# A hybrid decoder step on one core: when v is requested and used in the recurrence, and where small tiles and first triangles travel

## The chip, the core and the metric

The kernel runs on one core of a Trainium2 chip. The metric is device time in microseconds of one execution. A profiled execution leaves a trace with every instruction of the five engines: TensorE (PE, with its weight loads as PEld), VectorE (DVE), ScalarE (ACT), GpSimd (POOL), and SyncE (SP), which here only issues transfers (DMAs). ScalarE issues transfers too, in its own instruction order.

## The reference, cut to what matters

Two layers are computed, for a prompt of 2048 tokens with 16 learned meta tokens ahead, and for 8 short samples of 4 tokens. Layer 0 is sliding-window attention. Layer 1 is RWKV-7 time mixing with 16 heads of 64 channels, whose recurrence is, per token:

```
S = S * w_t + (S a_t) b_t^T + v_t k_t^T          # state, 64 x 64 per head
y_t = S r_t
...
y = (y - mean) * rsqrt(var + GN_EPS) * ln_g + ln_b      # per head
bonus = sum(r * k * r_k) * v
out = ((y + bonus) * silu(g)) @ w_out
```

The bonus is one number per token and head times v; it is added after the group norm.

## The kernel before, in words

The work is written in three phases: attention, the projections of the RWKV layer (their results go to DRAM), and the recurrence. The changes lie in the recurrence, which starts at some 1600 us.

**Units and chunks.** The recurrence runs over 17 units in order: unit 0 holds the meta tokens (one chunk of 32 tokens), units 1 to 16 hold 128 prompt tokens each, in four chunks of 32. Per chunk, `chain` (L1422) does on TensorE the products of the state Z with L (C<-Z,L), ScalarE copies them (R0s), the `solve` (L1394) multiplies by the inverted triangles TT (C<-R0s,TT), ScalarE writes the result into Z, TensorE multiplies by the keys LS (C<-Z,LS), and VectorE multiplies by the decay products `pe` and so writes the state of the next chunk (Z<-C,pe, L1464). These steps depend on each other in a ring. Half of each Z tile holds v of the chunk, loaded by SP two chunks ahead (`load_v`, L1367).

**What is made ahead.** For a unit two places later, `scores` (L948) multiplies BK with L into triangles LAs, `inverse` (L976) sends LAs to DRAM (la_d), loads it rearranged (LA) and inverts it in 31 small steps on GpSimd (X and XT), sends the result to DRAM (tt_d), and `load_TT` (L1334) brings it back as TT. `keys` (L1374) transposes BK on TensorE and ScalarE copies the result into LS. `load_BK` (L894) loads two tiles of 512 KB, `load_L` (L901) two halves of 256 KB for two chunks. The pool of L has six places, that of BK four.

**What follows behind.** `outputs` (L1465) forms y of two chunks (Y). `group_norm` (L1583) is a generator that does the group norm and the bonus of the previous unit in pieces, each ended by a mark. Its first piece requests v (vt<-v, two transfers on SP). Its second takes the mean of the first half and multiplies both vt tiles by the bonus (L1602, vt<-vt,bont). Further pieces subtract the mean, form the variance (VectorE sums, GpSimd's power of -1/2), and scale. `gate` (L1641) and `project_out` (L1684) are dense products that fill TensorE.

**The order of the work.** For units 2 to 14 the function `steady` (L1765) writes out for each of the four chunks which pieces are emitted in which order. At its end `in_order` (L1752) ties VectorE's, ScalarE's and GpSimd's instructions to the order in which they were written. The order of TensorE and SP is chosen by the framework's planner at build time, from simulated times; at run time every engine and queue goes strictly in order.

In chunk 3, `steady` creates the group norm of the unit and runs two pieces of it:

```
                else:
                    norms_[u.idx] = group_norm(u)
                    run(norms_[u.idx], to=MARK)
                    run(norms_[u.idx], to=MARK)
                run(pe[ch], 1.9)
                next(rec, None)
```

The last line emits C<-Z,LS and Z<-C,pe of the chunk. In chunks 0 to 2 the group norm of the previous unit advances by two marks each. BK and L are loaded through ScalarE's queue (`s_`): L of the first two chunks at the end of chunk 3 of the unit before (L1841, kept in `L0s`), BK and the other L at the end of chunk 0 (L1834).

The first three units (`PRE` = 3) are prepared by `elementwise` (L1340) and, for units 1 and 0, inside the projection phase. The small tiles `pe` and `bont` are loaded by `small_loads` (L1319) and lie in the pool `wk`, which belongs to the recurrence phase and takes room that the phase before has used; the pool `wp` (L660) is opened earlier and lives longer.

Of the kernel before, what the change touches and what calls it, by code (L numbers as in the profile page):

```python
# [10 lines left out]
F32 = mybir.dt.float32  # L11
# [3 lines left out]
ALU = mybir.AluOpType  # L15
# [4 lines left out]
P = 128  # L20
D = 1024
KC = 8
# [8 lines left out]
def tile_hybrid_step(ctx: ExitStack, tc: tile.TileContext, a, o, c):  # L31
    nc = tc.nc
    v_, s_, g_, t_ = nc.vector, nc.scalar, nc.gpsimd, nc.tensor
# [9 lines left out]
    def tt(e, out, in0, in1, op):  # L43
        return e.tensor_tensor(out=out, in0=in0, in1=in1, op=op).ins  # L44
# [4 lines left out]
    def dma(out, in_, eng=None):  # L49
        return (eng or nc.sync).dma_start(out=out, in_=in_).ins  # L50
# [192 lines left out]
    with ExitStack() as ph:  # L243
# [403 lines left out]
        n, off = ntok(NT), place[NT][1]  # L647
# [226 lines left out]
    def all_of(gen):  # L874
        for _ in gen:
            pass
# [17 lines left out]
    def load_BK(u, eng=None):  # L894
        u.BK, u.L = [], []
        for half in range(2):
            BK = es.tile([P, 4, 4, 64], F32, name="BK", tag="BK", bufs=nbuf["BK"])
            dma(BK, bk_d[u.blk][:, half * 4:half * 4 + 4, u.c0:u.c0 + u.nch, :], eng)
            u.BK.append(BK)
# [76 lines left out]
    def inverse(u, room=None, ln=None):  # L976

        nch = u.nch
        nl = nch * 16
        la_d = dramr.tile([2, nl // 2, 32, 32], F32, name="la_d", tag=f"la_d{nch}")  # L980
        u.tt_d = tt_d = dramr.tile([32, 4, 4 * nch * 32], F32, name="tt_d", tag=f"tt_d{nch}")
        for e in range(2):
            dma(la_d[e].rearrange("l j i -> j l i"),
                u.LAs[32 * e:32 * e + 32].rearrange("p h c g i -> p (h c g) i"))
        eng = v_ if u.idx == 1 else g_
        if u.kind == "m":
            room = wl.tile([P, 2, 32 * 32], F32, name="roomm", tag="L", bufs=nbuf["L"])
        if room is not None:
            LA = room[:, 0].rearrange("p (j i) -> p j i", i=32)
            XX = room[:, 1].rearrange("p (a k i) -> p a k i", a=2, i=32)  # L990
        else:

            LA = wk.tile([P, 32, 32], F32, name="LA", tag="LA", bufs=2)
            XX = None
        if XX is None:
            X = wk.tile([P, 16, 32], F32, name="X", tag="X", bufs=2)
            XT = wk.tile([P, 16, 32], F32, name="XT", tag="XT")
        else:
            X, XT = XX[:, 0], XX[:, 1]
        if ln is None:  # L1000
            ln = wp.tile([P, 32], F32, name="ln", tag=("mu", "rst0")[u.idx % 2])
        if nch < 4:
            g_.memset(LA, 0.0)
            g_.memset(ln, 1.0)
        for hh in range(2):
            dma(LA[hh * 64:hh * 64 + nl], la_d.rearrange("e l j i -> (e l) j i"))
            dma(ln[hh * 64:hh * 64 + nl], ln_d[u.idx].rearrange("q c g i -> (q c g) i"))
        tt(eng, LA, LA, ln.unsqueeze(2).broadcast_to([P, 32, 32]), ALU.mult)
        dma(X, c["laneid"])

        low = 16 if u.kind == "m" else 0

        part = {2: 16}.get(u.idx, 0)
        cut = [(v_, 0, part), (g_, part, 16)] if 0 < part < 16 else [(v_, 0, 16)] if part else [(eng, 0, 16)]
        for j in range(low, 31):
            if j in (8, 16, 22, 26):
                yield
            w = 3 - j % 4 if u.kind == "s" else 31 - j
            for eng, k0, k1 in cut if w else ():
                ks = slice(max(low // 2, k0), min(j // 2 + 1, k1))  # L1020
                shape = [P, ks.stop - ks.start, w]
                if shape[1] <= 0:
                    continue
                tt(eng, XT[:, ks, :w], LA[:, j:j + 1, j + 1:j + 1 + w].broadcast_to(shape), X[:, ks, j:j + 1].broadcast_to(shape), ALU.mult)
                tt(eng, X[:, ks, j + 1:j + 1 + w], X[:, ks, j + 1:j + 1 + w], XT[:, ks, :w], ALU.add)
        for eng, k0, k1 in reversed(cut):
            u.inverted = tt(eng, X[:, k0:k1], X[:, k0:k1], ln[:, None, :].broadcast_to([P, k1 - k0, 32]), ALU.mult)
        for hh in range(2):
            dma(tt_d[hh:32:2].rearrange("k q (l i) -> (q l) k i", i=32), X[hh * 64:hh * 64 + nl])
# [238 lines left out]
    with ExitStack() as ph:  # L1268
# [50 lines left out]
        def small_loads(u):  # L1319
            if u.kind == "s":  # L1320
                room = wp.tile([P, 192], F32, name="TTs", tag="l1_0")
                u.TT = room[:, 0:128].rearrange("p (c g i) -> p c g i", c=1, i=32)
                u.pe = room[:, 128:192].rearrange("p (g c) -> p g c", c=8)
            else:
                u.pe = wk.tile([P, KC, u.nch], F32, name="pe", tag="pe", bufs=4)
            dma(u.pe, pe_d[u.idx])
            if u.kind != "m":
                u.bont = wk.tile([P, 16], F32, name="bont", tag="bont", bufs=4)
                dma(u.bont[:u.n], bo_d[u.idx])

        def new_LAs(u):
# [80 lines left out]
        def run(gen, budget=None, to=None):  # L1412

            with released():
                while budget is None or budget > 0:
                    x = next(gen, None)
                    if x is None or (x == MARK and to == MARK):
                        return
                    if budget is not None and x != MARK:
                        budget -= x  # L1420
# [162 lines left out]
        def group_norm(u):  # L1583
# [12 lines left out]
            for x in range(2):  # L1596
                ms_ = mean[:n, x * 8:x * 8 + 8]
                v_.tensor_reduce(out=ms_, in_=u.Y[x][:n], axis=AX.X, op=ALU.add)
                v_.tensor_scalar(out=ms_, in0=ms_, scalar1=1.0 / 64, scalar2=None, op0=ALU.mult)
                if vts and x == 0:  # L1600
                    for e in range(2):
                        tt(v_, vts[e], vts[e], u.bont[:n, 8 - e * 8:16 - e * 8].unsqueeze(2).broadcast_to([n, 8, 64]), ALU.mult)  # L1602
                    yield MARK
                if x == 0:
                    u.ytm = u.Ys if u.kind == "s" else lt.tile([P, 2, 8, 64], F32, name="ytm", tag="ytm", bufs=1)
                    y = u.ytm[:n].rearrange("p e g d -> p (e g) d")
                for e, ps_ in HS:
                    if u.kind == "s" and e == 0:
                        tt(v_, u.ytm[:n, x], u.Y[x][:n], ms_.unsqueeze(2).broadcast_to([n, 8, 64]), ALU.subtract)
                    elif u.kind != "s":  # L1610
                        tt(v_, u.ytm[64 * x:64 * x + 64, e], u.Y[x][ps_],
                           mean[ps_, x * 8:x * 8 + 8].unsqueeze(2).broadcast_to([64, 8, 64]), ALU.subtract)
                yield MARK if vts and x == 0 else 2.3
# [6 lines left out]
            with tc.high_priority(offset=5000):  # L1620
                g_.tensor_scalar(out=var[:n], in0=var[:n], scalar1=1.0 / 64, scalar2=64e-5, op0=ALU.mult, op1=ALU.add)
                tt(g_, var[:n], var[:n], mhalf[:n], ALU.pow)
            yield MARK
            tt(v_, y, y, bc(var), ALU.mult)
            yield MARK
# [139 lines left out]
        def steady(i, u, pe):  # L1765
# [9 lines left out]
            for ch in range(4):  # L1775
# [36 lines left out]
                run(pe[ch], 1.2)  # L1812
                next(rec)
                with released():
                    if ch == 0 and i > 2:
                        all_of(keys(u, 1))
                    if ch == 3:
                        all_of(kt)
                        inv[s.idx] = inverse(s)
                        next(inv[s.idx])  # L1820
                    else:
                        next(inv.get(i + 1, idle()), None)
                if ch < 3:
                    run(norm, to=MARK)
                else:
                    norms_[u.idx] = group_norm(u)
                    run(norms_[u.idx], to=MARK)
                    run(norms_[u.idx], to=MARK)
                run(pe[ch], 1.9)
                next(rec, None)  # L1830
                with released():
                    if ch == 0:
                        first = L0s.pop(s.idx, None)
                        load_BK(s, s_)  # L1834
                        s.L.append(first or load_L(s, 0, s_))
                        s.L.append(load_L(s, 1, s_))
                        small_loads(s)
                    if ch == 2 and i + 1 in inv:
                        load_TT(us[i + 1])
                    if ch == 3 and i + 3 < len(us):  # L1840
                        L0s[i + 3] = load_L(us[i + 3], 0, s_)  # L1841
                run(pe[ch], to=MARK)
                rests.append(pe[ch])
                for part in PLAN.get((i, ch), ()):
                    with released():
# [214 lines left out]
```

## Time and profile before

| what | us |
|---|---|
| median of 3 runs | 2597.73 (2594.54 to 2601.28) |
| the profiled execution, its own time | 2601.98 |
| its span in the trace | 2600.2 |
| TensorE busy | 2238.5 (86%) |
| VectorE busy | 1687.0 (65%) |
| ScalarE busy | 1169.5 (45%) |
| GpSimd busy | 1044.8 (40%) |

The shares are means over phases with different limits. The page's slices show it: in the first 60% of the span TensorE stands at 9 tenths or more in most slices, and in the recurrence, from slice 25 on, at 5 to 8 tenths:

```
span 2600.2 us, 60852 instructions
PE   6999999899999898999999997567777777777897
POOL 4242123222112335433333333147566666656613
PEclk9999999999999998999999998778898988889999
```

In the rows below, "idle before <-X" in brackets is the time in which an engine had nothing to do just before the instruction, and what ended it. "issue" means that the profile shows nothing that the engine waited for. SPq and ACTq are transfers being issued by SP and ScalarE; the time is that of the issue, not of the transfer. Neighbouring instructions of one kind are merged into a row with their count.

### The profile page before, as it was taken

How to read it: one execution, taken by the hardware profiler on the slowest of the kernel's cores; microseconds unless marked ns; L12 is line 12 of the kernel's file. 1: busy time of each engine (PE TensorE's matmuls, PEld its weight loads, DVE VectorE, ACT ScalarE, POOL GpSimd, SP SyncE). 2: the span in 40 equal slices, each digit the busy share in tenths (PEclk: the TensorE clock that was granted, in tenths of full speed). 3: DMA queues.
4: the chain of work that ended last, by engine and by line, in shares of the span. 5: the costliest groups of instructions: out<-in, count | busy, mean ns of one | idle time of the engine just before them, and what ended most of it. 6: DMA issues, size and time to landing. Idle time of an engine off the chain costs nothing.

```text
span 2600.2 us, 60852 instructions
## 1 busy us (share of the span) xinstructions
PE 2238.5 (86%) x24932; PEld 1547.7 (60%) x24932; DVE 1687.0 (65%) x3181; ACT 1169.5 (45%) x2799; POOL 1044.8 (40%) x1572
## 2 busy tenths in 40 slices
PE   6999999899999898999999997567777777777897
PEld 5877777767845446676666785354444444444553
DVE  7586675567749887665656665645666566666684
ACT  6676455555523335454434444233443434434432
POOL 4242123222112335433333333147566666656613
PEclk9999999999999998999999998778898988889999
DMA  8433122331447664322222216564544545454423
GB/s 202 122 106 117 63 69 94 107 115 62 150 138 226 210 205 153 98 81 96 86 102 85 93 67 192 140 182 118 132 105 114 135 115 131 103 126 124 106 67 76
DMA packets 346235, 312.99 MB, mean 120 GB/s; under 512 B 205546, under 2 KB 282218, under 8 KB 344131
## 3 DMA queue, kind: packets, MB, share of 16 engines
q1 hardware_dynamic: 327219, 278.03, 36.4%
q10 hardware_dynamic: 17120, 27.27, 4.0%
q0 software_dynamic: 1616, 3.79, 0.7%
q8 instruction: 196, 3.21, 0.5%
q14 instruction: 84, 0.69, 0.1%
HBM read 191.15 MB, written 119.84 MB: 120 GB/s over the span
## 4 chain that ended last, share of the span: by engine, by line
PE 50%; DVE 18%; issue 10%; ACT 9%; DMA 8%; POOL 4%; SPq 2%; POOLq 0%; ACTq 0%; DVEq 0%
PE pd L38 29%; PE po L38 5%; PE C L38 5%; DVE xm L47 4%; DMA BK<-bk 2%; DVE xpr L44 2%; ACT ssb L41 2%; PE pz L38 2%; SPq L50 2%; PE Y L38 2%; PE sc L38 1%; PE oT L38 1%; DMA wst<-in_rwkv_w_in 1%; DMA L<-ar 1%; PE kt L1385 1%
## 5 line engine op out<-in xcount | busy, mean ns | idle before, releaser
L38 PEld LDWEIGHTS <-yp 128*128 128x128 f16 x1488 | 141.1, 99 | 165.2 <-issue 12.8
L47 DVE SCALAR_TENSOR_TENSOR xm<-dx,mu,xn 128x256 f32<-128x256 f32 (+2 forms) x432 | 199.8, 523 | 48.9 <-POOL dx L44 47.6
L44 POOL TENSOR_TENSOR X<-X,XT 128x126 f32<-128x126 f32 (+24 forms) x458 | 202.4, 442 | 35.5
L44 POOL TENSOR_TENSOR XT<-LA,X 128x126 f32<-128x126 f32 (+24 forms) x458 | 180.4, 394 | 39.7 <-DVE X L44 6.0
L38 PE MATMUL C<-Z,L 128*32 128x64 f32 x2048 | 49.5, 247 | 170.4 <-issue 159.9
L38 PE MATMUL pd<-xp,wq 128*128 128x256 f16 (+2 forms) x1728 | 186.0, 266 | 11.4 <-DVE qp L47 8.0
L38 PE MATMUL pd<-wg,xg 128*128 128x512 f16 (+1 forms) x816 | 193.1, 384 | 0.7 <-issue 0.7
L38 PE MATMUL po<-wo,yp 128*128 128x512 f16 x768 | 188.9, 389 | 0.0
L38 PE MATMUL pd<-wvv,xpr 128*128 128x512 f16 (+1 forms) x816 | 187.4, 387 | 0.0
L38 PE MATMUL pd<-xpr,w 128*128 128x256 f16 (+2 forms) x1728 | 186.0, 267 | 0.0
L38 PE MATMUL pd<-xp,wg 128*128 128x256 f16 (+2 forms) x1728 | 182.6, 266 | 0.9 <-DVE xp L44 0.5
L38 PE MATMUL pd<-xpr,wkk 128*128 128x256 f16 (+2 forms) x1728 | 179.5, 264 | 0.0
L38 PEld LDWEIGHTS <-wq 128*128 128x128 f16 x1728 | 159.3, 99 | 32.7 <-DVE qp L47 9.2
L44 POOL TENSOR_TENSOR ssb<-ssb,bias 128x512 f32<-128x512 f32 x64 | 86.4, 1355 | 223.9 <-DVE ssb L462 185.5
L38 PEld LDWEIGHTS <-w 128*128 128x128 f16 x1728 | 157.5, 99 | 27.0 <-issue 9.7
L38 PEld LDWEIGHTS <-wg 128*128 128x128 f16 x1728 | 159.2, 99 | 21.5 <-issue 4.0
L38 PEld LDWEIGHTS <-wkk 128*128 128x128 f16 x1728 | 158.2, 98 | 15.6 <-issue 0.4
L38 PE MATMUL pd<-w,yp 128*128 128x512 f16 x720 | 162.9, 384 | 3.3 <-DMA yp<-y 3.3
L44 POOL TENSOR_TENSOR ps<-wst,ps 128x1024 f16<-128x1024 f32 x32 | 69.5, 2171 | 220.0 <-ACT wst L41 201.7
L38 PEld LDWEIGHTS C<-Z,L 128*32 128x32 f32 x2048 | 38.9, 126 | 195.8 <-issue 192.3
L41 ACT ACTIVATE R0s<-C 128x256 f32<-128x256 f32 x65 | 25.0, 385 | 274.9 <-PE C L38 269.9
L38 PEld LDWEIGHTS <-xpr 128*128 128x128 f16 (+1 forms) x816 | 79.1, 100 | 102.6 <-issue 17.5
(357 smaller groups left out, 4913.2 us busy)
## 6 DMA issues: line engine op xcount, KB each, us to landing
wst<-in_rwkv_w_in SPq DMA_DIRECT2D x32, 512.0 KB
wsp<-ps SPq DMA_DIRECT2D x32, 512.0 KB
x<-in_x_prompt SPq DMA_DIRECT2D x29, 512.0 KB
xn<-xn SPq DMA_DIRECT2D x14, 1028.0 KB
ar<-aro SPq DMA_DIRECT2D x28, 512.0 KB
bk<-bko SPq DMA_DIRECT2D x28, 512.0 KB
BK<-bk ACTq DMA_DIRECT2D x26, 512.0 KB
L<-ar ACTq DMA_DIRECT2D x52, 256.0 KB
```

The source lines that it names most:

```text
L38: return t_.matmul(out=out, lhsT=lhsT, rhs=rhs, start=start, stop=stop, **kw).ins
L41: return s_.activation(out=out, in_=in_, func=func, **kw).ins
L44: return e.tensor_tensor(out=out, in0=in0, in1=in1, op=op).ins
L47: v_.scalar_tensor_tensor(out=out, in0=in0, scalar=scalar, in1=in1, op0=op0, op1=op1)
L50: return (eng or nc.sync).dma_start(out=out, in_=in_).ins
L1385: t_.transpose(out=ps[:w * 64, j].rearrange("p e d -> p (e d)"), in_=u.BK[half][:, j, 2 * c2:2 * c2 + w, :].rearrange("p c x -> p (c x)"), ...
```

## The change

Six things are edited.

1. The two multiplications of vt by the bonus leave the second piece of `group_norm` and form a piece of their own behind the variance's power and ahead of the scaling.
2. `steady` creates the group norm of a unit and runs its first piece (the request for v) at the end of chunk 2 instead of in chunk 3; chunk 3 runs one piece, and at the end of chunk 0 one more piece of the previous unit's norm is run, which is the new one.
3. BK and the first L of the unit two places later are loaded in chunk 0 through SP, between the transposes of the keys and their copies, instead of through ScalarE at the end of chunk 0. The second L stays with ScalarE.
4. The lines that load the first L of a later unit (`if ch == 3 and i + 3 < len(us)`) keep their indentation and so come to lie inside `if ch == 2`.
5. `pe` and `bont` get places in the pool `wp` instead of `wk`.
6. For units 0 to 2 the transfers la_d<-LAs and LA<-la_d are issued by ScalarE instead of SP.

```diff
@@ inverse
         for e in range(2):
             dma(la_d[e].rearrange("l j i -> j l i"),
-                u.LAs[32 * e:32 * e + 32].rearrange("p h c g i -> p (h c g) i"))
+                u.LAs[32 * e:32 * e + 32].rearrange("p h c g i -> p (h c g) i"), s_ if u.idx < PRE else None)
...
         for hh in range(2):
-            dma(LA[hh * 64:hh * 64 + nl], la_d.rearrange("e l j i -> (e l) j i"))
+            dma(LA[hh * 64:hh * 64 + nl], la_d.rearrange("e l j i -> (e l) j i"), s_ if u.idx < PRE else None)
@@ small_loads
-                u.pe = wk.tile([P, KC, u.nch], F32, name="pe", tag="pe", bufs=4)
+                u.pe = wp.tile([P, KC, u.nch], F32, name="pe", tag="pe", bufs=4)
...
-                u.bont = wk.tile([P, 16], F32, name="bont", tag="bont", bufs=4)
+                u.bont = wp.tile([P, 16], F32, name="bont", tag="bont", bufs=4)
@@ group_norm
                 if vts and x == 0:
-                    for e in range(2):
-                        tt(v_, vts[e], vts[e], u.bont[:n, 8 - e * 8:16 - e * 8].unsqueeze(2).broadcast_to([n, 8, 64]), ALU.mult)
                     yield MARK
...
                 tt(g_, var[:n], var[:n], mhalf[:n], ALU.pow)
+            yield MARK
+            for e, vt in enumerate(vts):
+                tt(v_, vt, vt, u.bont[:n, 8 - e * 8:16 - e * 8].unsqueeze(2).broadcast_to([n, 8, 64]), ALU.mult)
             yield MARK
             tt(v_, y, y, bc(var), ALU.mult)
@@ steady
                 with released():
-                    if ch == 0 and i > 2:
-                        all_of(keys(u, 1))
+                    if ch == 0:
+                        kt = keys(u, 1) if i > 2 else idle()
+                        next(kt, None)
+                        first = L0s.pop(s.idx, None)
+                        load_BK(s)
+                        s.L.append(first or load_L(s, 0))
+                        all_of(kt)
...
                 else:
-                    norms_[u.idx] = group_norm(u)
-                    run(norms_[u.idx], to=MARK)
                     run(norms_[u.idx], to=MARK)
                 run(pe[ch], 1.9)
                 next(rec, None)
                 with released():
                     if ch == 0:
-                        first = L0s.pop(s.idx, None)
-                        load_BK(s, s_)
-                        s.L.append(first or load_L(s, 0, s_))
                         s.L.append(load_L(s, 1, s_))
                         small_loads(s)
                     if ch == 2 and i + 1 in inv:
                         load_TT(us[i + 1])
+                if ch == 2:
+                    norms_[u.idx] = group_norm(u)
+                    run(norms_[u.idx], to=MARK)
                     if ch == 3 and i + 3 < len(us):
                         L0s[i + 3] = load_L(us[i + 3], 0, s_)
                 run(pe[ch], to=MARK)
+                if ch == 0:
+                    run(norm, to=MARK)
```

## Rows read from the trace of the kernel before

**Rows 1.** Waits from 1700 to 2400 us: engine, line, releaser, total us, times, longest.

```profile
POOL LA L44 <- DMA LA<-la_d: 120.2, 13, 33.6
DVE vt L44 <- DMA vt<-v: 116.1, 26, 7.7
POOL var L1621 <- DVE var L1618: 76.2, 11, 7.7
```

**Rows 2.** Windows, one unit: length, busy PE, PEld, DVE, ACT, POOL; PEclk, DMA, GB/s.

```profile
2019.80:2072.60 52.80, 39.60 (x762) 24.53 (x760) 32.94 (x50) 21.20 (x54) 33.75 (x69) 0.90 0.48 122
```

**Rows 3.** Chain of waits in order of time, 1560 to 2560: start, us, what.

```profile
1716.65 12.21 DMA L<-ar
...
1808.64 9.06 issue
...
2344.12 8.02 issue
```

**Rows 4.** Timeline of all engines around one unit's end: start, us, engine, instruction.

```profile
2013.02 1.35 SPq L50 DMA_DIRECT2D tt_d<-X  x2
...
2014.48 1.91 SPq L50 DMA_DIRECT2D LA<-la_d  x2
...
2017.67 1.09 SPq L50 DMA_DIRECT2D TT<-tt_d  x2
...
2018.39 1.15 PE L38 MATMUL C<-Z,LS 128*64 128x64 f32 x32
...
2019.27 0.66 SPq L50 DMA_DIRECT2D out_y_prompt<-h  x1
...
2020.31 2.01 DVE L44 TENSOR_TENSOR vt<-vt,bont 128x512 f32<-128x512 f32 x1 [2.93 <-DMA vt<-v]
...
2029.45 0.79 DVE L44 TENSOR_TENSOR vt<-vt,bont 128x512 f32<-128x512 f32 x1 [7.13 <-DMA vt<-v]
...
2030.17 1.72 DVE L44 TENSOR_TENSOR Z<-C,pe 64x256 f32<-64x256 f32 x4
...
2030.69 0.32 SPq L50 DMA_DIRECT2D h<-h  x1
...
2031.99 1.08 PE L38 MATMUL C<-Z,L 128*32 128x64 f32 x32 [10.40 <-issue]
...
2034.70 0.82 PE L38 MATMUL C<-R0s,TT 32*32 32x64 f32 x32
```

**Rows 5.** Timeline of TensorE, matmuls: the first product of successive chunks.

```profile
1749.20 0.65 PE L38 MATMUL C<-Z,L 128*32 128x64 f32 x32
...
1759.01 0.65 PE L38 MATMUL C<-Z,L 128*32 128x64 f32 x32 [0.58 <-PE pd L38]
...
1770.77 0.65 PE L38 MATMUL C<-Z,L 128*32 128x64 f32 x32 [1.55 <-issue]
...
2205.25 0.65 PE L38 MATMUL C<-Z,L 128*32 128x64 f32 x32 [1.55 <-issue]
...
2215.32 0.65 PE L38 MATMUL C<-Z,L 128*32 128x64 f32 x32
...
2225.10 0.65 PE L38 MATMUL C<-Z,L 128*32 128x64 f32 x32
```

**Rows 6.** Timeline of GpSimd: starts of the inverse's first step.

```profile
1760.00 2.28 POOL L44 TENSOR_TENSOR LA<-LA,ln 128x1024 f32<-128x1024 f32 x1 [33.61 <-DMA LA<-la_d]
...
1805.37 1.91 POOL L44 TENSOR_TENSOR LA<-LA,ln 128x1024 f32<-128x1024 f32 x1 [6.76 <-DMA LA<-la_d]
...
2394.75 1.91 POOL L44 TENSOR_TENSOR LA<-LA,ln 128x1024 f32<-128x1024 f32 x1 [6.98 <-DMA LA<-la_d]
```

**Rows 7.** Timeline in chunk 0 and 1 of a steady unit: BK's issue and use.

```profile
2040.34 0.37 ACTq L50 DMA_DIRECT2D BK<-bk  x1
...
2047.69 0.69 PE L38 MATMUL pz<-L,BK 64*64 64x64 f32 x32 [1.26 <-DMA BK<-bk]
```

**Rows 8.** Timeline of VectorE at the recurrence's start.

```profile
1653.74 1.73 DVE L44 TENSOR_TENSOR Z<-C,pe 64x256 f32<-64x256 f32 x4 [7.97 <-DMA pe<-pe]
```

## The prediction

> **What bounds the kernel now.** I read the waits first, summed over the stretch in which most of the recurrence's steady units run [rows 1]. VectorE's multiplication of v by the bonus (vt<-vt,bont) waits 116.1 us for its transfer, 26 times, and GpSimd stands 120.2 us for LA and 76.2 us for VectorE's variance. One unit by the windows [rows 2]: in 52.8 us TensorE is busy 39.60, VectorE 32.94, GpSimd 33.75. No engine is full; what ends a unit is an order.
>
> The chain of waits in order of time shows the place [rows 3]: once a unit TensorE stands in "issue", from 9.06 us at 1808.64 to 8.02 us at 2344.12, 11 such pieces, 8 to 12 us each. The timeline of one such end of a unit explains it [rows 4]. The last LS products of chunk 3 end at 2019.54 (2018.39 + 1.15). VectorE could then make the next Z, but it works in written order, and ahead of Z<-C,pe stand the two bonus multiplications: the first waits 2.93 us and starts at 2020.31, the second waits 7.13 us and starts at 2029.45. Only then comes Z (2030.17, first piece), and with it the next unit's first chunk (C<-Z,L at 2031.99).
>
> Where vt happened to be in time, the same boundary is short [rows 5]: chunk 3 starts at 1749.20 and the next unit at 1759.01, 9.81 us. Chunk 0 then takes 11.76 (to 1770.77), chunk 1 10.07 and chunk 2 9.78 (2205.25, 2215.32, 2225.10). A unit of TensorE without the stand is 9.81 + 11.76 + 10.07 + 9.78 = 41.4 us, waits for BK included.
>
> GpSimd has a loop of its own, one triangle inverse a unit [rows 6]. LA starts at 1760.00 and 1805.37: 45.4 us, a loop in which the variance was not waited for. From 1805.37 to 2394.75 eleven loops take 589.4, 53.58 each; they hold the variance wait, 76.2 / 11 = 6.9 us [rows 1]. Without it they are 46.7. So GpSimd cannot do a unit in less than 45.4 to 46.7 us as long as LA's load stands on SP behind tt_d<-X, the end of the previous inverse (2013.02, then 2014.48) [rows 4]; the wait for that load was 6.76 us in the short loop too.
>
> **The change, part by part.**
>
> *v later and requested sooner.* The bonus multiplications leave the end of chunk 3 for the end of the next unit's chunk 0, behind Z; the request for v goes from the end of chunk 3 to the end of chunk 2. Of the old place only the mean remains ahead of Z. So 11 stands of about 10 us go: Z can start at about 2019.6 and take 1.7 us, the next unit starts near 2021.6 instead of 2031.99, 10.4 us sooner. At the new place v has had a whole chunk 3 and chunk 0, over 20 us, against the 10 us and a little that its second half now takes (requested just ahead of the output row's issue at 2019.27, used at 2029.45) [rows 4]. The two instructions cost VectorE 0.79 us each when alone and 2.01 beside GpSimd's LA product; their cover is VectorE's idle 19.9 us of 52.8, some 13 of 46 afterwards [rows 2, 4].
>
> *What is late next.* TensorE's loop falls to 41.4, GpSimd's to 46 (the middle of 45.4 and 46.7: the variance comes 10 us sooner and is no longer waited for). GpSimd is slower, and its result reaches TensorE: X's end lets tt_d go (2013.02), TT is loaded at 2017.67, and the solve of the next unit's chunk 0 reads it, now at 2034.70. With the next unit at 2021.6 that solve comes by 2024.3: still after TT in the first such unit, but GpSimd loses 46.0 - 41.4 = 4.6 us a unit, so from the second on TensorE waits there for TT. I take 46.0 a unit: 11 x (53.58 - 46.0) = 83 us.
>
> *The page "SBUF — State Buffer" of the Trainium skill, section "Who interferes with whom", speaks against this part:* a VectorE instruction with two inputs in SBUF and a GpSimd instruction that reads SBUF block each other, the later one for the whole of the earlier. The 2.01 us beside the LA product agrees. By that rule the moved pair falls among GpSimd's steps; what this would give is priced as a rival from rows.
>
> *BK and the first L.* They go from ScalarE's queue to SP's, ahead of the copies of the keys instead of behind. The prefetch of the first L at the end of the previous unit is moved under a condition that cannot hold (chunk 3 inside chunk 2), so it is gone: L's 0.5 MB is now loaded in chunk 0 beside BK's 1 MB and the second L's 0.5 MB. Now BK is issued 8.35 us after the unit's start (2040.34 against 2031.99) and the scores wait 1.26 us for it at 2047.69 [rows 4, 7]. Lower bound of the change: -1.3 us a unit (no wait left). Upper: unit 2 loads both L and BK in chunk 0 today, and L lands 12.21 us after its issue [rows 3]; issued 8.35 us after the start at the latest, that is 20.6 against a need at 11.8, an 8.8 us wait a unit. I take 2 us, near the row of the ordinary unit since SP issues about 1 us sooner; TensorE's loop becomes 43.4, still under 46, so nothing is added. The cover is the wait for TT; gone that, it costs those 2 us. ScalarE sheds four issues a unit, worth nothing (it is not the bound).
>
> *Places of their own, first triangles on ScalarE's queue.* The first decay products arrive 7.97 us late at VectorE (1653.74) [rows 8]. A place that shares no earlier tile lets them be fetched long before; behind that wait stand the transfer of Z's v half and TT, so 0 to 8 us, I take 4. The triangles of units 0 to 2 leave SP's queue; between nothing and some of the same 8 us, taken as inside it. From the third unit on both edits are at nothing.
>
> Sum: 83 + 4 = 87 us from the profiled execution's 2601.98 (span 2600.2): 2515. The median of the runs, 2597.73, is 0.16% below that execution; on its scale 2510.
>
> **Rivals.**
>
> 1. *TensorE bounds, LA gets ahead of tt_d.* The order on SP is planned anew. With the scores 10 us sooner, LA's triangle is in DRAM well before X ends, and if LA's load is put first, the 7 us wait goes and GpSimd's loop is about 39. Then TensorE's 41.4 to 43.4 counts, say 42: 11 x 11.6 + 4 = 131 us, 2467. Against it: in the short loop the triangle was early too, and LA still waited 6.76 us [rows 6].
>
> 2. *GpSimd's steps stand behind the moved pair.* Two multiplications of 0.79 us held against its chain make its loop 46.0 + 1.6 = 47.6: 11 x 6.0 + 4 = 70 us, 2528. For it: the 2.01 us in rows 4 show the two engines holding each other. Against: the 45.4 and 46.7 already hold such meetings.
>
> 3. *The transfers of chunk 0 bound.* L as in unit 2, an 8.8 us wait in place of 1: 41.4 - 1.0 + 8.8 = 49.2: 11 x 4.4 + 4 = 52 us, 2542. Without the 4 and at a still later L it ends near 2597, no change.
>
> 4. *Slower: BK and L stand behind h on SP.* The load of h waits until the previous output row is out: issued 2019.27, h at 2030.69 [rows 4]. With the next unit at 2021.6 that is 9.1 us into it, and BK and L now queue behind it. By their tile shapes h, xg, Z's v, BK and both L are 3.25 MB; at unit 2's pace (2 MB in 12.2 us) 19.8 us, so landing 28.9 us into the unit against a need at 11.8: a 17.1 us wait, loop 57.5, 11 x 3.9 = 43 us slower, 2641. It decides from a wait of 13.2 us (53.58 - 40.4). Against it: v's 0.5 MB and L's 0.5 MB leave the very stretch in which that output row is slow, and TensorE's wait for TT gives time back.
>
> **How the numbers follow.** Forecast 0.49 (its own range 2498 to 2524, from loops of 45.4 to 46.7 and 0 to 8 us at the start), rival 1 0.20, rival 2 0.10, rival 3 0.12, rival 4 0.06, no change in effect 0.03. About 0.3% (8 us) is what runs of this kernel can tell from no change. Faster by more: 0.49 + 0.20 + 0.10 + 0.12 = 0.91; within 0.03; slower 0.06. The range takes in the forecast, rivals 1 and 2 and most of 3: 2455 to 2560.
>
> **What would show it.** Right: the wait of vt for v gone from VectorE; the 11 long "issue" pieces gone; LA starts on GpSimd 45 to 47 us apart with the variance not waited for; a new wait of the chunk-0 solve for TT of some 3 us. Rival 1: LA issued ahead of tt_d and a loop near 42. Rival 2: a 46 us chain stretched by steps of over 1 us beside vt. Rivals 3 and 4: long waits of the scores for BK or L. The prediction is wrong if units stay above 49 us or fall under 43.

## The result and the profile after

The changed kernel takes 2566.14 us (median of 4 runs, 2564.59 to 2570.74), the kernel before, on the same chip, 2596.14 (2592.95 to 2601.28): ratio 0.9886, 95% interval 0.9864 to 0.9907. It is 30 us faster; 87 were forecast, and the time lies 6 us above the range. The profiled executions have spans of 2562.7 us and 2600.2.

The waits from 1700 to 2400 us, columns as in [rows 1]:

```profile
POOL LA L44 <- DMA LA<-la_d: 73.2, 7, 11.8
...
PEld pz L38 <- issue: 55.4, 18, 5.9
PE pz L38 <- DMA BK<-bk: 49.7, 17, 5.5
...
PE C L38 <- DMA TT<-tt_d: 26.7, 17, 2.7
...
POOL ms L1704 <- ACT po L41: 13.1, 6, 3.2
```

VectorE's wait of vt is gone, and so is GpSimd's for the variance. What is new stands on TensorE: the scores wait for BK (the weight loads beside them show the same time as "issue"), and the solve waits for TT. GpSimd's wait for LA is larger than this row says: six more of its starts are put down to other transfers that landed last, or to "issue". For the scores' wait for BK the same view of the kernel before has this:

```profile
PE pz L38 <- DMA BK<-bk: 9.1, 8, 2.3
```

The starts of the inverse on GpSimd, first and last of twelve on the changed kernel's timeline, answer to [rows 6]:

```profile
1811.64 1.91 POOL L44 TENSOR_TENSOR LA<-LA,ln 128x1024 f32<-128x1024 f32 x1 [9.24 <-DMA LA<-la_d]
...
2359.18 1.92 POOL L44 TENSOR_TENSOR LA<-LA,ln 128x1024 f32<-128x1024 f32 x1 [8.18 <-issue]
```

Eleven loops take 547.5 us, 49.8 each, where 53.6 were and 46.0 forecast; the wait ahead of them is 10.3 us on average (7.3 before). 11 x 3.8 = 42 us came from the loops; the first of these starts is 6.3 us later than in [rows 6], and the stretch behind the last takes some 2 us less: 37.5 in the spans.

One unit's end by the timeline of all engines of the changed kernel answers to [rows 4] (the last row is the scores of the next unit's chunk 1):

```profile
2142.79 1.55 ACT L41 ACTIVATE LAs<-pz 32x256 f32<-32x256 f32 x4 [0.91 <-PE pz L38]
...
2144.88 1.46 SPq L50 DMA_DIRECT2D Z<-v  x1
2146.44 0.97 SPq L50 DMA_DIRECT2D la_d<-LAs  x2
2146.59 1.64 POOL L44 TENSOR_TENSOR X<-X,ln 128x512 f32<-128x512 f32 x1
2147.47 0.63 SPq L50 DMA_DIRECT2D L<-ar  x1
2148.26 1.34 SPq L50 DMA_DIRECT2D tt_d<-X  x2
2149.71 1.21 SPq L50 DMA_DIRECT2D LA<-la_d  x1
...
2151.01 1.01 SPq L50 DMA_DIRECT2D vt<-v  x2
2152.07 0.48 SPq L50 DMA_DIRECT2D LA<-la_d  x1
...
2152.66 1.10 SPq L50 DMA_DIRECT2D TT<-tt_d  x2
2153.81 0.49 SPq L50 DMA_DIRECT2D L<-ar  x1
...
2159.14 1.92 POOL L44 TENSOR_TENSOR LA<-LA,ln 128x1024 f32<-128x1024 f32 x1 [10.90 <-DMA out_y_prompt<-h]
2159.78 0.65 PE L38 MATMUL C<-Z,L 128*32 128x64 f32 x32
...
2163.03 0.64 PE L38 MATMUL C<-R0s,TT 32*32 32x64 f32 x28 [1.47 <-DMA TT<-tt_d]
...
2165.14 0.32 SPq L50 DMA_DIRECT2D h<-h  x1
...
2168.05 3.81 SPq L50 DMA_DIRECT2D BK<-bk  x2
...
2178.43 1.25 PE L38 MATMUL pz<-L,BK 64*64 64x64 f32 x32 [4.48 <-DMA BK<-bk]
```

The next unit now starts with no stand ahead of it (2159.78; 10.40 us in [rows 4]). But SP's line has changed: the first half of L lies between la_d and tt_d, v between the two halves of LA, and BK goes out behind h, which waits for the output row. The chain of waits names the new links, where "issue" stood in [rows 3]; here is one round of it:

```profile
2103.05 9.34 DMA TT<-tt_d
...
2120.71 9.33 DMA BK<-bk
...
2141.26 0.62 ACT po L41 x2
...
2141.96 0.20 POOL ms L1704
...
2148.94 3.66 DMA tt_d<-X
2153.24 9.74 DMA TT<-tt_d
...
2169.71 10.88 DMA BK<-bk
```

**A ring of one unit.** These rows close a ring, from TT at 2103.05 to the next TT at 2153.24, 50.2 us. TT reaches the solve of chunk 0; the scores of chunk 1 wait for BK; in chunk 2 ScalarE sums the squares (po) from which GpSimd makes ms, the factor of the final norm; ms stands among the inverse's last steps, and the inverse's end lets tt_d and the next TT go. In other units SP itself is the link from chunk 2 to tt_d: the loads of Z's v half wait there for TensorE, and la_d and tt_d stand behind them. Between 1800 and 2360 us the changed kernel's chain goes round this ring through TensorE in seven units, from 2003 on; in the three before it goes round GpSimd's own loop (LA, inverse, tt_d, LA).

**Four links.** A longer ring can be laid over two units: the inverse ends and TT reaches the solve (2148.23 to 2163.03); from there chunks 0 to 2 up to the last LAs; la_d and LA up to GpSimd's start; the inverse; and then TT again, for the unit after next. I took the four from the timelines of all units between 1800 and 2350 us, as means. Two loops hold the four links by construction, so half their sum is the loop (within 0.4 us, since not every unit has all four) whichever ring sets it; what the table tells is which link is long. The changed kernel's chain nowhere runs all four in a row.

| kernel | inverse's end to solve | solve to last LAs | LAs to inverse | inverse | half the sum |
|---|---|---|---|---|---|
| before | 22.2 | 25.2 | 13.3 | 46.1 | 53.4 |
| after | 14.7 | 31.1 | 14.4 | 39.5 | 49.8 |
| e2 | 14.4 | 30.4 | 11.5 | 40.5 | 48.5 |
| e3 | 15.8 | 28.4 | 11.9 | 40.3 | 48.2 |
| e10 | 14.5 | 25.9 | 11.8 | 42.3 | 47.2 |
| e16 | 14.9 | 30.3 | 14.3 | 39.6 | 49.6 |
| e15 | 14.0 | 27.8 | 19.4 | 43.3 | 52.3 |
| e17 | 14.6 | 31.8 | 11.1 | 42.7 | 50.1 |
| e18 | 14.7 | 28.0 | 11.7 | 41.3 | 47.9 |

Before, the first link held some 7 us of slack (TT was there before the solve came) and the inverse 6.9 us of waiting for the variance. After, both are gone: TensorE waits for TT, GpSimd waits for LA and, in six of the eleven inverses, for ms as well.

### The profile page after: what moved, and what is told of

The parts are those of the page before. It is cut to its first block, busy times and chain, and to the rows that moved or that the text cites. A ratio compares the mean times of both kernels' runs of the same rounds, so it can differ in the third digit from the quotient of the medians.

```text
span 2562.7 us, 60891 instructions
## 1 busy us (share of the span) xinstructions
PE 2245.7 (88%) x24932; PEld 1544.6 (60%) x24932; DVE 1681.5 (66%) x3181; ACT 1168.8 (46%) x2799; POOL 1041.8 (41%) x1572
## 4 chain that ended last, share of the span: by engine, by line
PE 33%; DVE 19%; DMA 17%; POOL 10%; ACT 9%; issue 8%; SPq 4%; ACTq 0%; POOLq 0%; DVEq 0%
PE pd L38 19%; PE po L38 5%; DVE xm L47 5%; SPq L50 4%; DMA BK<-bk 3%; DMA TT<-tt_d 3%; POOL X L44 3%; PE C L38 2%; DVE xpr L44 2%; POOL XT L44 2%; ACT ssb L41 2%; DMA wst<-in_rwkv_w_in 2%; DMA tt_d<-X 1%; PE pz L38 1%; DMA x<-in_x_prompt 1%
## 5 line engine op out<-in xcount | busy, mean ns | idle before, releaser
L44 POOL TENSOR_TENSOR X<-X,XT 128x126 f32<-128x126 f32 (+24 forms) x458 | 196.9, 430 | 35.7
L38 PE MATMUL po<-wo,yp 128*128 128x512 f16 x768 | 201.5, 408 | 0.0
L44 POOL TENSOR_TENSOR XT<-LA,X 128x126 f32<-128x126 f32 (+24 forms) x458 | 175.8, 384 | 40.4 <-issue 6.7
L44 DVE TENSOR_TENSOR Z<-C,pe 64x256 f32<-64x256 f32 x256 | 108.0, 422 | 68.4 <-PE C L38 53.0
L44 DVE TENSOR_TENSOR xpr<-xm,xpr 128x512 f16<-128x512 f32 (+2 forms) x144 | 98.9, 708 | 55.2 <-ACT xpr L41 54.8
L41 ACT ACTIVATE ssb<-ssb,ng 128x128 f32<-128x128 f32 (+1 forms) x272 | 104.2, 384 | 57.0 <-DVE es L44 53.4
```

The costliest lines, as they stand in the source:

```text
L38: return t_.matmul(out=out, lhsT=lhsT, rhs=rhs, start=start, stop=stop, **kw).ins
L41: return s_.activation(out=out, in_=in_, func=func, **kw).ins
```

## The experiments

Ratios are to the kernel before, with 95% intervals; loops are those of GpSimd's starts. The edits are shown shortened.

**Parts of the change taken back: e1, e2, e3, e4.**

e2 requests v in chunk 3 again and still uses it late; e1 loads BK and both L through ScalarE again; e3 does both; e4 is the kernel before with edits 5 and 6 alone.

```diff
 e2, steady                              e1, steady
-  if ch == 2: norms_[u.idx] = group_norm(u); run(to=MARK)
+  (ch == 3)   norms_[u.idx] = group_norm(u); run(to=MARK)     # e2
-  load_BK(s); s.L.append(first or load_L(s, 0))               # between keys' halves
+  load_BK(s, s_); s.L.append(first or load_L(s, 0, s_))       # e1, end of chunk 0
```

> BK and both L go back to ScalarE's queue at their old places, the early load of the first L included; v and the rest stay as changed. Theory 1 (two limits nearly equal in the changed kernel: GpSimd's loop of 49.8 us a unit with a 10.4 us wait for LA, and TensorE's of some 49 us with a 5 us wait for BK issued behind h on SP): the wait for BK falls under 2 us, but GpSimd still waits 8 to 10 us for LA because v is requested among its loads; about 2545 to 2560. Theory 2 (LA's wait alone binds): 2560 to 2570, no change. Theory 3 (BK's wait alone binds): about 2510 to 2525.

> Only the request for v goes back to chunk 3; it is still used late, and BK and L stay on SP. Theory 1: LA's wait falls from 10.4 towards 7 us, BK's wait stays at 5 us and TensorE's loop of 49 us binds; 2550 to 2566. Theory 2: 11 x 3.4 us less, about 2525. Theory 3: no change, 2560 to 2570.

> The request for v and the loads of BK and L all go back to their old places: what remains of the change is that v is used late, and the places at the start. Theory 1: both waits fall, loops of about 46 us, 2515 to 2530, which is what was predicted for the whole change. Theories 2 and 3 expect the same here. If it stays above 2550, v's and L's transfers at the end of chunk 3 slow LA in any order, and the transfers themselves bind.

> The kernel before with two edits of the change alone: places of their own for pe and bont, and the first units' la_d and LA transfers issued by ScalarE. Nothing in the steady units changes. The prediction gave them 4 us, between 0 and 8: 2588 to 2600. The changed kernel's own trace has its first chunk of unit 1 9.5 us and that of unit 3 6.3 us sooner than before; if these edits alone are the cause, 2588 to 2594.

e2 took 2555.69 us (0.9827, 0.9802 to 0.9853), e3 2546.02 (0.9785, 0.9764 to 0.9806), e4 2597.96 (1.0000, 0.9982 to 1.0018), e1 2637.65 (1.0143, 1.0119 to 1.0167). So neither request change paid here: the late use of v alone, e3, is faster than the whole change. v's early request costs 2.9 us between LAs and the inverse (14.4 against 11.5), of which 1.4 come out in the loop (49.8 against 48.4): GpSimd waits longer for ms instead, and e2's chain of waits passes TT and BK in its units and LA in none. With BK and L on SP the way from solve to LAs is 2 us longer (30.4 against 28.4), but the loops of e2 and e3 are nearly the same (48.4 and 48.2) and their intervals touch, so what these two loads cost is left open.

e1 is slower for another reason than the one it was made for. With BK and L gone from SP, the planner gave SP another order, with both v transfers ahead of LA, as the timeline of one unit's end shows:

```profile
2023.92 1.36 SPq L50 DMA_DIRECT2D tt_d<-X  x2
2025.37 1.70 SPq L50 DMA_DIRECT2D vt<-v  x2
2027.16 0.49 SPq L50 DMA_DIRECT2D LA<-la_d  x1
2028.59 1.11 SPq L50 DMA_DIRECT2D TT<-tt_d  x2
2029.75 0.50 SPq L50 DMA_DIRECT2D LA<-la_d  x1
2030.30 0.58 SPq L50 DMA_DIRECT2D out_y_prompt<-h  x1
2041.38 1.91 POOL L44 TENSOR_TENSOR LA<-LA,ln 128x1024 f32<-128x1024 f32 x1 [17.48 <-DMA LA<-la_d]
```

The wait for LA is 16.3 us and the loop 55.4. It therefore says nothing of BK and L by themselves.

e4: the first product of the recurrence starts 8.4 us sooner, but the first triangles' inverses start later on (1669.79 and 1692.17 against 1660.80 and 1685.13), and unit 3 starts 1.8 us later than before (1760.85 against 1759.01 in [rows 5]). The early start is lost on the way. ScalarE's queue is one part of it: there LA of the first of these inverses is issued at 1660.57, on SP before at 1655.25. The second one's transfers stay on SP, so its delay has another reason, which no run isolates.

**Other queues and places: e5, e6, e7, e8.**

```diff
 e5: - s_ if u.idx < PRE else None      + s_          # la_d, LA of all units on ScalarE
 e6: + yield MARK                       # ahead of ms in project_out (e7: the same on e3)
 e8 (on e7): v requested behind the variance, multiplied just ahead of the add
```

> In all units, not only the first three, la_d<-LAs and LA<-la_d are issued by ScalarE, so LA's load no longer stands behind tt_d<-X on SP. Theory 1: GpSimd's wait for LA falls to a few us, TensorE's loop with the BK wait (about 49 us) binds; 2545 to 2560. Theory 2: GpSimd's loop falls to 42 to 45 us, 2500 to 2520. Theory 3: no change. A cost of its own: ScalarE stands 2 to 4 us for la_d's write in chunk 3, ahead of the next unit's R0s, which could give back up to 4 us a unit.

> The changed kernel; only GpSimd's three small instructions for the final norm of the unit before (ms) are emitted one mark later, so they stand behind the end of the inverse instead of ahead of its last steps. Theory R (the unit is a ring through two engines: X's end, tt_d and TT through DRAM 14.8 us, from the solve over TensorE's chunks 0 and 1 to the sum of squares that ms waits for 29.8 us, from ms to X's end 6.3 us, together the 50.9 us of the loop): the link between TensorE and GpSimd in chunk 2 is cut, GpSimd's own loop of about 48.6 us is left, 20 to 25 us less than the changed kernel, about 2540 to 2548. Theory 2 (LA's wait on GpSimd alone binds): what GpSimd saves at ms it waits more for LA, 2560 to 2570.

> As e3_both_back (2546 us: v requested and BK and L loaded at the old places, v used late), and ms one mark later. Theory R: the ring of e3 (15.8 + 27.2 + 6.3 = 49.2 us) is cut, GpSimd's loop of 45.8 to 46.7 us is left, which is the loop that was predicted: 11 x 2 to 2.5 us less, 2515 to 2525. Theory 2: no change, 2540 to 2550.

> As e7_both_ms, and v is requested only behind the variance (chunk 0 of the next unit by the written order) and multiplied by the bonus just ahead of its addition; on SP the request stands behind TT's and LA's loads. Theory R with the transfers as the price of its first link: LA's wait falls from 7.6 to some 5 us and TT lands earlier, loops of 44 to 45 us, 2490 to 2512. Theory 2: LA's wait falls by the same, 11 x 2.5 us under e3, 2515 to 2525. A cost of its own: VectorE waits for vt in chunk 2 if the transfer takes over 20 us.

e5, e6 and e7 were slower than what they were made from, e8 faster than e7 but slower than e3: e5 2732.76 (1.0501, 1.0473 to 1.0529), e6 2666.58 (1.0255, 1.0236 to 1.0274), e7 2649.92 (1.0197, 1.0175 to 1.0220), e8 2630.0 (1.0115, 1.0084 to 1.0145). In e5, LA's load stands in ScalarE's written order in chunk 3 and holds ScalarE until la_d is out (10 us in the unit at 2143); GpSimd waits some 24 us for LA. From 2150 us on, SP's timeline in e6 shows another place: the planner put the store of LAs behind that of X, and LA's load behind TT and v:

```profile
2152.03 1.34 SPq L50 DMA_DIRECT2D tt_d<-X  x2
2153.47 2.42 SPq L50 DMA_DIRECT2D la_d<-LAs  x2
...
2159.42 1.15 SPq L50 DMA_DIRECT2D LA<-la_d  x2
```

LAs was complete at 2145.8, and its store waits there for the inverse's end (GpSimd's last product starts at 2150.74). The wait for LA is 18.6 us, the loop 57.6. In e7 and e8 la_d stands behind tt_d too, with waits of 18.2 and 16.6. So ms' wait was not tested by these. What they show is that an edit in the code is also an edit of SP's order. That this order, and not the edit, costs the time is argued from the wait for LA; no run has e6's edit with the old order.

**LA ahead of X's store: e9, e10, e12, e13.** From here on, in all but e11, the order on SP was written out as dependencies. e9 (on e3) and e10 (on the changed kernel) store la_d from ScalarE in chunk 2 and issue LA ahead of tt_d, v behind it. e12 is e10 with a piece of the inverse ended four steps later, so that GpSimd comes to the variance later; e13 is e12 with three more multiplications on GpSimd, and v held behind tt_d, where it stood.

```diff
 e9, e10: + tc.add_manual_dep(tt_d_store, LA_load.name, NoSync)      # la_d by s_, in chunk 2
 e12: - if j in (8, 16, 22, 26): yield    + if j in (8, 20, 22, 26): yield
 e13: + for _ in range(3): tt(g_, XT, LA[:, :16], ln..., ALU.mult)   # ahead of the last product
```

> The kernel with both request changes taken back (2546.0 us), with three things more for units 2 to 14: la_d is stored by ScalarE in chunk 2, right behind the copies that make LAs, LA's load is written there too, and SP issues it ahead of tt_d and of v. In the kernel it is made from, LAs is complete 6 us before the inverse ends, la_d waits on SP behind small loads and LA behind tt_d, and GpSimd starts 7.6 us after the end. Theory A, the two units' ring (TT lands, solve of chunk 0, scores of chunk 2, LAs, la_d, LA, 41 us of inverse, tt_d, TT of the unit after next; 96.4 us for two units): LA lands 4 to 5 us sooner, GpSimd waits about 3 us, and a unit gets half of the gain, 2 to 2.5 us: loop 46, 11 x 2.3 = 25 us, 2521. Rival, GpSimd's own loop bounds alone: a unit gets all of it, 44, 2496. Rival, the loop is set by TT and the scores without LA: GpSimd's wait only moves, loop 48.2, 2546.

> The same three things on the changed kernel itself (2566.1 us, loop 49.8, GpSimd's wait for LA 10.4 us). Theory A: LA lands some 6 us sooner, a unit gets half, 3 us: loop 46.8, 2533, and the waits for BK (some 5 us a unit) stay. Rival, GpSimd alone: 44, 2502. Rival, BK's wait sets the loop: 49.8, 2566.

> The kernel of e10 (2546.5 us, loop 47.45; GpSimd waits 5.0 us for LA and 3.4 us for the variance), with the second piece of the inverse ended at step 20 instead of 16, so that GpSimd does four steps (some 3.5 us) more before it comes to the variance. Theory, one-unit ring (TT, chunk 0, variance, rest of the inverse, tt_d, TT; 10 + 3.1 + 19.3 + 14.6 = 47): its rest of the inverse gets 3.4 us shorter; what then binds is the two-unit ring, 25 + 12.5 + 39 + 14.6 = 91, 45.6 a unit: 11 x 1.85 = 20 us, 2526. Rival, GpSimd alone: loop 39 + 5 = 44, 2509. Rival, VectorE stands for the later variance and holds Z back: no gain or slower, 2546 to 2560.

> e12 with three more multiplications on GpSimd just ahead of the inverse's last product (scratch results, not used; order on SP as in e12), some 3 x 0.7 to 1.3 us a unit. Two-unit ring: a unit gets half of the added time, 1 to 2 us, and GpSimd's wait for LA shrinks by the other half. GpSimd alone: all of it, 2 to 4 us, and the wait stays. A ring without GpSimd: nothing, the wait shrinks by all of it.

e9 took 2557.98 (0.9844, 0.9820 to 0.9867), slower than e3 though the wait for LA fell from 7.7 to 4.3; the variance is waited for instead. e10 took 2546.53 (0.9798, 0.9771 to 0.9826), loop 47.5 with a wait of 5.0. The waits for BK, expected to stay, are gone there (none over 0.2 us) though BK still stands behind h on SP; TensorE waits for TT instead (56.2 us from 1700 to 2400, 26.7 in the changed kernel). e12, 2557.22 (0.9820, 0.9793 to 0.9848), missed: the variance's wait went, the one for LA rose to 8.7. e13 says why. It took 2552.02 (0.9812, 0.9780 to 0.9843), no more than e12, with 4.7 us of work added to each inverse, here at the end of one on GpSimd's timeline:

```profile
2148.44 4.69 POOL L44 TENSOR_TENSOR XT<-LA,ln 128x512 f32<-128x512 f32 x3
2153.09 1.27 POOL L44 TENSOR_TENSOR X<-X,ln 128x512 f32<-128x512 f32 x1
2158.68 1.91 POOL L44 TENSOR_TENSOR LA<-LA,ln 128x1024 f32<-128x1024 f32 x1 [4.32 <-DMA LA<-la_d]
```

The loop is 48.7 against 48.9, and the wait for LA 3.5 against 8.7: it took in all of the added work. In this order GpSimd has slack, and a ring of one unit without the inverse sets the loop, LAs, la_d, LA, tt_d, TT, solve: in e12 the inverse ended at 2142.25, and tt_d went out at 2146.84, behind LA at 2145.65, which waited for la_d.

**The changed kernel's own order: e16, e15, e17.** e16 writes out its order on SP as the control; e15 adds e13's three multiplications; e17 moves v and both halves of L behind TT.

```diff
 e16: + chained([*la_d, L[0], *tt_d, LA[0], *v, LA[1], *TT, L[1]])
 e15: the same, + for _ in range(3): tt(g_, XT, ...)
 e17: + chained([*la_d, *tt_d, *LA, *TT, *v, *L])
```

> The changed kernel with the order of its transfers on SP written out as dependencies, as its trace shows it (la_d, half of L, tt_d, half of LA, v, half of LA, TT, half of L; pe moves ahead of la_d). The control for the next two: 2566 us, loop 49.8, GpSimd's wait for LA 10.3, within 5 us; every theory expects that.

> The same order, and three more multiplications on GpSimd ahead of the inverse's last product (scratch results, not used), about 3 x 1.65 = 5 us a unit. Two-unit ring (TT, chunks 0 to 2, LAs, la_d, LA, inverse, tt_d, TT of the unit after next): loop 49.8 + 2.5 = 52.3, wait for LA 7.8, 11 x 2.5 = 27 us, 2593. GpSimd alone, with a wait that is the same whatever else happens: loop 54.8, wait 10.3, 2621. Ring without the inverse: loop 49.8, wait 5.3, 2566.

> The same as the control, but v and both halves of L are issued behind TT: la_d, tt_d, LA, TT, v, L. If these three transfers of 1 MB are what delays LA and TT: wait for LA 7 to 8 us, TT 1 to 2 us sooner, and by the two-unit ring the loop falls by half of the sum, 2 us, to 47.8: 2544; by GpSimd alone by 3 us, 46.8: 2533. If LA and TT are slow for their own sake: 49.8, 2566.

The control took 2568.91 (0.9895, 0.9870 to 0.9920), loop 49.6: as the changed kernel. e15 took 2593.31 (0.9988, 0.9966 to 1.0010), loop 51.9: of 4.7 us, 2.3 came out. That is near the half that the ring of two units expects, and not the whole that GpSimd alone does, nor nothing. But it is no proof of that ring: the last of the eleven loops (44.3) has no wait for LA, and over the first ten 3.1 came out. Nor is the order quite the control's: what the list doesn't name moved, bont ahead of tt_d and the second half of L behind the output row. And the waits are not all as expected: that for LA fell only to 8.3, that of the scores for BK vanished, and the solve's for TT grew. Rows of e15's waits from 1700 to 2400 us, and behind them one of SP's own:

```profile
PE C L38 <- DMA TT<-tt_d: 89.3, 26, 8.1
POOL LA L44 <- DMA LA<-la_d: 74.5, 9, 9.4
...
PE pz L38 <- DMA BK<-bk: 9.6, 8, 1.7
```

```profile
SPq L50 <- POOL X L44: 71.4, 13, 10.0
```

TensorE came to have slack, and GpSimd with LA's load behind tt_d took over as the bound: tt_d waits on SP for the inverse's end in every unit (5 times and 16.3 us in the same stretch of the changed kernel), and the chain's last five loops are GpSimd's own. Taking the added 4.7 us off the 52.7 of the first ten loops, GpSimd's own loop in the control is some 48, an estimate, where its loop is 49.6. So GpSimd had a little slack there, part of it in front of ms, and the added work used it up before it came out. In the control's chain LA and the whole inverse stand twice between two solves, so the longer ring is close behind there.

e17 took 2574.90 (0.9917, 0.9890 to 0.9945). Its step worked and its sum did not: the wait for LA fell from 9.9 to 7.7, as expected, yet the loop rose to 50.4. What GpSimd gained at LA it lost at ms, which waits for TensorE's chunk 2; the waits from 1700 to 2400 us, first of the control, then of e17:

```profile
POOL ms L1711 <- ACT po L41: 17.5, 7, 3.6
```

```profile
POOL ms L1711 <- ACT po L41: 62.0, 11, 7.3
```

Between 1800 and 2360 us e17's chain of waits passes TT ten times, BK eleven times and LA never: the ring of one unit sets its loop, and an earlier LA gives nothing. In that ring BK is waited for longer, 61.1 us against 40.8 in the control. The output row now leaves behind v and L, h waits for it, and BK stands behind h, in the timeline of e17:

```profile
2112.81 0.53 SPq L50 DMA_DIRECT2D out_y_prompt<-h  x1
...
2124.28 0.33 SPq L50 DMA_DIRECT2D h<-h  x1
...
2127.18 3.26 SPq L50 DMA_DIRECT2D BK<-bk  x2
...
2139.12 1.13 PE L38 MATMUL pz<-L,BK 64*64 64x64 f32 x32 [7.48 <-DMA BK<-bk]
```

That is not all of it: as a mean BK's first issue comes 9.9 us into e17's units and 9.5 into the control's.

**Versions to keep: e11, e14, e18.** e11 is e3 with the first triangles on SP again, e14 the same for e12. e18 is e11 with SP's order la_d, tt_d, LA, TT, v, pe, bont written out: BK and L don't stand behind h there.

> The kernel with both request changes taken back (2546.0 us), and the first units' la_d and LA by SP again; pe and bont keep their own places. In the kernel before plus the two start edits the first product began 8.4 us sooner, but unit 3 began 1.8 us later: the first triangles' inverses started 7 to 9 us later than before (1669.79 against 1660.80, 1692.17 against 1685.13). If ScalarE's queue is what delays them, unit 3 starts 6 to 8 us sooner now and the time is 2539; if they are late for the transfers' own sake, it stays at 2546; if SP is held by them ahead of what the first unit needs, the first product starts later again and the time is 2546 to 2552.

> e12 with the first units' la_d and LA by SP again (e11: -3.6 us with an interval that reaches zero). If the start is worth what e11's median says: 4 us under e12. If not, the same as e12.

> The kernel of e11 (2542.4 us, loop 48.0, wait for LA 7.2) with SP's order written out as la_d, tt_d, LA, TT, v, and pe and bont behind v. There tt_d stood 1.4 us behind pe and bont, and TT 0.6 to 1.3 us behind v. Two-unit ring: 2 us off LAs to LA and off the end of the inverse to TT together, or more if v's 0.5 MB slows them, so 1 to 2 us a unit: 2520 to 2531. If the transfers are slow for their own sake or another place takes it up: 2542.

e11 took 2542.40 (0.9787, 0.9753 to 0.9821), which can't be told from e3, and e14 2544.04 (0.9787, 0.9745 to 0.9829), whose interval touches that of e12. e18 took 2532.13 (0.9743, 0.9712 to 0.9774): it beats the kernel before by 2.6% and the changed one, whose interval starts at 0.9864. Its loop of 47.8 is only 0.2 under e11's, less than the 1 us expected; the rest of its lead over e11 is within what these intervals leave open. Its waits for LA, after the first (27.3), are 6 to 8 us, and BK is waited for little (waits, 1700 to 2400 us):

```profile
POOL LA L44 <- DMA LA<-la_d: 100.6, 12, 27.3
...
PE C L38 <- DMA TT<-tt_d: 24.3, 12, 4.4
PE pz L38 <- DMA BK<-bk: 20.7, 15, 2.2
```

## Why the prediction was right in sign and wrong in size

- **The stand at vt goes.** Right: the wait and the long "issue" pieces at the units' ends are gone, and so is the variance's wait. e3, which keeps only the late use and the start edits, gets all of the gain and more.
- **What is late next: TT, through GpSimd.** Right as a place: the solve waits for TT, 1.47 us in the unit shown, where some 3 were forecast.
- **"TensorE's loop becomes 43.4, still under 46, so nothing is added."** This step failed. TensorE's loop came to 49.8, and in the changed kernel's chain of waits it, and not GpSimd's, sets seven of ten units. BK and L were given 2 us of waiting; from 1800 to 2350 us the scores wait 4.5 us a unit for BK (0.6 before), and the way from solve to LAs is 5.9 us longer in all. And the loop was laid along TensorE's chunks alone, as if TT could only be late when GpSimd lags: TT's way of 14.7 us begins behind chunk 2 of the unit, by ms or by SP's line, and so it belongs to TensorE's loop.
- **What the loops fell short by.** By the links the ring of one unit is 14.7 from the inverse's end to the solve, 31.1 on to the last LAs and 4.0 from there to the inverse's end, together 49.8. With the 25.2 that the middle link had before it would be 43.9, close to the 43.4, and GpSimd's loop would have been the longer. So comparing two loops is not what failed, but TensorE's was sized 6 us too short: 49.8 - 46.0 is 3.8 us a unit, 11 x 3.8 = 42 us, and the loops fell short by 41. Of the 5.9, about 4 are BK's longer wait; the rest I did not trace. BK is not issued later in the unit (2168.05 - 2159.78 = 8.3 us, 8.35 before), but its two issues take 3.81 us, in which SP waits for TensorE, and the scores start 10.4 us after the first, where at most 7.35 passed in [rows 7]. What makes the transfer longer no run isolates.
- **GpSimd's 46** was too short as well: the wait for LA, carried over from [rows 6] as 7 us, is 10.3 with v between LA's halves, and e15 puts GpSimd's own loop at some 48.
- **The start: +4 taken, 0 measured** (e4). In the changed kernel unit 3 starts 6.3 us sooner (1752.68), but GpSimd's inverse beside it 3.6 us later (1763.57 against 1760.00 in [rows 6]); VectorE waits there 16.88 us for GpSimd's variance, and the first steady inverse starts 6.3 us later than before. "The triangles leave SP's queue ... taken as inside it" left out that they can come later from ScalarE's queue, by 5.3 us in e4.
- **The rivals.** Rival 1 (LA ahead of tt_d) is what e9 and e10 build, and the 2467 it promised isn't there: LA waits for la_d, and tt_d then waits behind LA. Rival 2 isn't seen: without the variance's wait the inverse had 39.2 us, now it has 39.5, with the waits for ms in it. (The 0.79 us taken as that of the pair alone stood beside a GpSimd product too, which took 0.71 us at 2029.78, with 0.38 to 0.43 for those next to it.) Rival 3 has the right kind of loop and nearly its length (49.2), but by luck: it took 40.4 without the wait and 8.8 for it, where the links give 43.9 and 5.9. Rival 4's order, BK behind h behind the output row, is in the changed kernel's trace, but BK's issue is no later than before, and some 5 us of waiting came where 13 to 17 were priced. The need "at 11.8" in both is the start of chunk 1; in [rows 7] the scores need BK at 14.4 (2047.69 - 1.26 - 2031.99), so their waits were over 2 us too long from the outset.

## What to carry to other kernels

When two engines hand work to each other through transfers, the way of the transfer belongs to the loop of each, and so do the transfers that stand ahead of it on the same queue and what these wait for. A wait seen today is not a cost that stays: e17 took 2 us off one wait, and another took them up. When an order on one queue is planned anew at every build, read the new order of the transfers first, before the edit's own gain is counted; e6, with LA's store behind X's, is 100 us slower than the changed kernel, and its longer wait for LA (18.6 against 10.3) is most of that. Moving a use later was worth more than asking for its data sooner.

## What the runs showed of the hardware

A result of 256 KB that goes through DRAM from GpSimd's last product to TensorE's solve took 14.0 to 15.8 us as a mean in all the kernels of the table in which TensorE waited for it, with their different orders of transfers: tt_d to TT's issue some 4 us and TT's issue to its use some 10 (2148.26, 2152.66, 2163.03). No edit of the table brought it under 14.0.
